# A decoder trunk on one core: groups of a projection unit no longer chained to the unit ahead, and three measured durations in the planner

## The chip, the cores and the metric

The kernel runs on one core of a Trainium2 chip. The metric is device time in microseconds (us), the median of several executions. Beside it there is one profiled execution with its trace; times "at 103.77" are us from the start of that trace's span. TensorE is called PE, its weight loads PEld, VectorE DVE, ScalarE ACT, GpSimd POOL, and the engine that issues the DMAs SP.

## The reference

Two layers over 256 tokens of width 1024. A layer normalises its input, multiplies it by one wide matrix (9808 columns), runs three causal attention mixers of 8 heads of 64 over the result, gates and projects each, merges them and adds the output projection to the residual.

```
for layer in range(2):
    h = rms_norm(x, gain)
    proj = h @ w_in                                # 1024 x 9808
    qa,ka,va,ga, qb,kb,vb,gb, qc,kc,vc,gc, q_idx,k_idx,w_idx, f_logit, merge = split(proj)
    oa = softmax(rope(qa) rope(ka)^T / 8 + causal) va * silu(ga)
    ob = the same for b, over the 64 keys that the indexer (q_idx, k_idx, w_idx) selects
    oc = the same for c without rope, with a bias of summed log_sigmoid(f_logit)
    merged = sum over n of sigmoid(merge[n]) * (o[n] @ w_branch[n])
    x = x + merged @ w_out
out = rms_norm(x, final_gain)
```

## The kernel before

Every fp32 product is made of three matmuls of rounded parts: an operand is split into a high part (`hi`, a copy on ACT) and the rest (`lo`, a subtraction on DVE), and hi x hi, hi x lo and lo x hi are summed in one PSUM bank. Weights come by DMA into one of three `raw` buffers; a piece of 128 columns (or of 2 rows of 128 by 512) is split into `wh` and `wl`, each a ring of six buffers.

The work is written as **units**. A unit of `unit_b` multiplies 128 columns of `w_in` by the transposed input `hTh`/`hTl` (256 tokens): 24 matmuls of 256 columns into one of three `proj` banks, 16 that need only `wh` and 8 that need `wl`. `unit_a` (values `v..`, output projection `o..`) and `unit_y` (branch projections `y..`) have 24 and 12 matmuls. Names: `ka2` is the key unit of mixer a for the pair of heads 2, `ga2` its gate unit, `qc2`, `gc2` likewise for mixer c; `m06` is a merge gate; `o00` and `o01` are the first two output units. A unit is issued in **groups** (`mm_ops`): before, 8, 5, 8 and 3 matmuls in `unit_b`, with `wl` needed from the second group on.

Between the units PE does the attention steps of a pair: the scores (`qk`, `scores`, six matmuls into both `s` banks), two sets of three transposes of the softmaxed scores (`pT`), and the product with the values (`av`). What they need is made on ACT and DVE: head-wise copies of queries and keys (`write_q`, `write_bd`, 64 partitions high), the maximum scan (L651), the exponential (L655), the normalisation (L663 on ACT or L666 on DVE), the copies of the transposes (L681, L683).

The order on every engine is made by a **planner** (`Plan.run`) while the program is built. Each operation has its tokens read and written, a key (its unit's number) and a duration from a formula. The planner takes the engine that can begin something first, and on it the operation that can begin first; among those that can begin at that moment, the lowest key. What it takes is fixed: the engines run their lists in order and wait by semaphores. Buffers of a ring are given in the order in which they are first named.

In the kernel before, every `mm_ops` call that belongs to a unit also writes one token, `k_main`, so that each group follows the group ahead of it, over unit borders too:

```
pe(emit, cost * n, reads, writes + ([k_main] if main else []), key, name)
```

Of the kernel before, what the change touches and what calls it, by code (L numbers as in the profile page):

```python
# [11 lines left out]
AF = mybir.ActivationFunctionType  # L12
# [3 lines left out]
S = 256  # L16
# [20 lines left out]
       ("ACT", "PE"): 170.0, ("DVE", "PE"): 200.0, ("POOL", "PE"): 170.0,  # L37
       ("DVE", "DVE"): 127.0, ("ACT", "ACT"): 127.0, ("POOL", "POOL"): 100.0, ("ACT", "SP"): 1500.0, ("DVE", "SP"): 1500.0}
SEM = 70.0
HALF = 95.0  # L40
SPLIT_LEAD = 2.0
MARGIN = 200.0
QK_MARGIN = 1000.0
# [3 lines left out]
DMA_KEY = (-95, -94, -85, -84)  # L47
HI_KEY = (-60, -48, -47, -46)
NB1 = 2
EARLY = 1.5  # L50
HT_KEY = (-50, -49.5, -46.8, -46.2)
BANKS = ("proj", "s", "t", "o")
# [176 lines left out]
def t_mm(n):  # L229
    return 1.3 + 0.4434 * n  # L230
# [3 lines left out]
def hybrid_trunk(ctx, tc, x, norm_gain, w_in, forget_bias, w_branch, w_out, final_gain, consts, out):  # L234
    nc = tc.nc
    PE, ACT, DVE, POOL = nc.tensor, nc.scalar, nc.vector, nc.gpsimd
# [17 lines left out]
    def pe(fn, cost, reads, writes, key, name="", margin=0.0, touch=()):  # L254
        o = plan.op([("PE", cost, fn)], reads, writes, key, 0.0, name, touch)
        o.margin = margin
        return o
# [52 lines left out]
    ncs = pool.tile([128, 2, 8], F32, name="ncs")  # L310
    widx = pool.tile([128, 2, 8], F32, name="widx")

    k_id, k_rope, k_gT, k_bdz, k_cst, k_fb, k_wf, k_widx, k_lf, k_cs, k_main = (Tok() for _ in range(11))
    k_cT, k_row = Tok(), [Tok() for _ in range(6)]
    k_isc = [Tok() for _ in range(2)]
    k_selb = [Tok() for _ in range(2)]
# [83 lines left out]
            dve(lambda: DVE.scalar_tensor_tensor(lo(), src(), scale, hi().bitcast(F32), op0=ALU.mult,  # L400
                                                 op1=ALU.subtract), n, reads + [wh], [wl], key, name, port=not ps)

    def mm_ops(o, terms, cost, writes, key, name, first, last, main=False):

        n = len(terms)

        def emit():
            for i, (a, b, _) in enumerate(terms):
                PE.matmul(o(), a(), b(), start=first and i == 0, stop=last and i == n - 1)  # L409
        reads = list({id(r): r for t in terms for r in t[2]}.values())  # L410
        pe(emit, cost * n, reads, writes + ([k_main] if main else []), key, name)

    units = [0]

# [6 lines left out]
    def unit_b(name, get, npart=128):  # L421
        u = unit(name)
        p = get(u)
        ps = Buf("proj")
        o = lambda: T(ps)[:npart, :S]
        his = [(lambda k=k: p[0].v[:, k], lambda k=k, h=h: h[:, k], [p[0]] + hT_all[i])
               for k in range(KC) for i, h in enumerate((hTh, hTl))]
        los = [(lambda k=k: p[1].v[:, k], lambda k=k: hTh[:, k], [p[1]] + hT_all[0]) for k in range(KC)]
        g = his[:8] + los[:2] + his[8:11] + los[2:5] + his[11:] + los[5:]
        for a, b in ((0, 8), (8, 13), (13, 21), (21, 24)):  # L430
            mm_ops(o, g[a:b], t_mm(256), [ps], u, name, a == 0, b == 24, True)
        return u, ps

    def unit_a(name, gets, t, ah, al, ra, c=0, n=512):
        u = unit(name)
        ps = Buf("proj")
        o = lambda: T(ps)[:, :n]
        for i in range(4):
            p = gets[i](u)
            g = []  # L440
            for k in (2 * i, 2 * i + 1):
                wh = lambda p=p, k=k: p[0].v[:, k % 2, c:c + n]
                g += [(lambda k=k: ah(k, t), wh, [p[0]] + ra[0](k)), (lambda k=k: al(k, t), wh, [p[0]] + ra[1](k))]
            for k in (2 * i, 2 * i + 1):
                wl = lambda p=p, k=k: p[1].v[:, k % 2, c:c + n]
                g += [(lambda k=k: ah(k, t), wl, [p[1]] + ra[0](k))]
            mm_ops(o, g, t_mm(n), [ps], u, name, i == 0, i == 3, True)
        return u, ps

    def rope(ps, key, np_=128):  # L450
# [119 lines left out]
    def write_q(src, n_ps, key, scale=None, name="q"):  # L570

        q = Buf("qh"), Buf("qx"), Buf("qy")
        up, dn = slice(0, 64), slice(64, 128)
        split_to(lambda: T(q[0]), lambda: T(q[2]), src[0], S, n_ps, [src[1]], q[0], q[2], key, scale, name)
        kx = [Tok(), Tok()]
        for t, o, a, b, i in ((q[1], up, q[0], up, 0), (q[1], dn, q[2], up, 1), (q[2], up, q[0], dn, None)):
            act(lambda t=t, o=o, a=a, b=b: ACT.activation(T(t)[o], T(a)[b].bitcast(F32), AF.Copy), S, False, [a],
                [q[2]] if i is None else [kx[i]], key, name, HALF, touch=[t])
        return q, kx

    def scores(q, k, ktoks, key, margin=MARGIN, shared=False):
        s0, s1 = Buf("s"), Buf("s")
        kt = [t for h in ktoks for t in h]
        q, kx = q

        def go():
            qh, x = T(q[0]), [T(q[1]), T(q[2])]
            kh, kl = T(k)
            for o, sl, n in ((T(s0)[:, :256], slice(0, 128), 128), (T(s1), slice(128, 256), 256)):
                PE.matmul(o.rearrange("p (h c) -> p h c", h=2), qh[:, sl], kl[:, :, :n], start=True, stop=False)  # L590
                for h in range(2):
                    PE.matmul(o[:, h * n:(h + 1) * n], x[h][:, sl], kh[:, 0 if shared else h, :n], start=False, stop=h == 1)  # L592
        pe(go, 3 * t_mm(256) + t_mm(512) + 216.0, [q[0], q[1], q[2], k] + kx + kt, [s0, s1], key, "qk", margin)
        return s0, s1

    class Pair:
# [44 lines left out]
        def attend(self, key):  # L641
# [31 lines left out]
            for h in range(2):  # L673
                ps = Buf("t")

                def tr(h=h, ps=ps):
                    for i in range(3):
                        PE.transpose(T(ps)[:, i * 128:(i + 1) * 128], T(es[h])[:, i * 128:(i + 1) * 128], ident)  # L678
                pe(tr, 330.0, ke[h] + [k_id], [ps], key, "pT", MARGIN, touch=[es[h]])
                src = lambda ps=ps: T(ps)[:, :384]  # L680
                act(lambda h=h, src=src: ACT.activation(T(ph)[:, h], src(), AF.Copy), 384, True, [ps],  # L681
                    [kp[h][0]], key, "pT", touch=[ph])
                dve(lambda h=h, src=src: DVE.tensor_tensor(T(pl)[:, h], src(), T(ph)[:, h].bitcast(F32), op=ALU.subtract),  # L683
                    384, [ps, kp[h][0]], [kp[h][1]], key, "pT", touch=[ph, pl])
# [41 lines left out]
    def write_bd(src, b, toks, key, ps, shared=False):  # L726

        up, dn = slice(0, 64), slice(64, 128)
        for h, o in enumerate((up, dn)):
            g, x = (0, up) if shared else (h, o)  # L730
            s = lambda x=x: T(src)[x, :S]
            hi = lambda x=x, g=g: T(b)[0][x, g]
            lo = lambda o=o, h=h: T(b)[1][o, h]
            if not (shared and h):
                act(lambda hi=hi, s=s: ACT.activation(hi(), s(), AF.Copy), S, ps, [src], [toks[g][0]], key, "bd", HALF, touch=[b])
                y = dn if x is up else up
                act(lambda hi=hi, y=y, g=g: ACT.activation(T(b)[0][y, g], hi().bitcast(F32), AF.Copy), S, False, [toks[g][0]],
                    [toks[g][1]], key, "bd", HALF, touch=[b])
            dve(lambda hi=hi, lo=lo, s=s: DVE.tensor_tensor(lo(), s(), hi().bitcast(F32), op=ALU.subtract), S,
                [src, k_bdz, toks[g][0]], [toks[h][2]], key, "bd", t_dve(S) + HALF, touch=[b], port=not ps)  # L740

# [125 lines left out]
    def unit_y(l, n, j, oi, gates, rank):  # L867
        u = unit(f"y{n}{j}")
        p = wbr(l, n, j, u)
        ps = Buf("proj")  # L870
        gh, gl = og[oi]
        cs = slice((j % 2) * 128, (j % 2) * 128 + 128)
        o = lambda: T(ps)[:, :S]
        g = []
        for k in range(4):
            wh, wl = lambda k=k: p[0].v[:, k, cs], lambda k=k: p[1].v[:, k, cs]
            g += [(wh, lambda k=k: gh[:, k], [p[0], k_og[oi][0][k]]), (wh, lambda k=k: gl[:, k], [p[0], k_og[oi][1][k]]),
                  (wl, lambda k=k: gh[:, k], [p[1], k_og[oi][0][k]])]
        g = [g[i] for i in (0, 1, 3, 2, 4, 5, 6, 7, 9, 10, 8, 11)]
        for a in (0, 6):  # L880
            mm_ops(o, g[a:a + 6], t_mm(256), [ps], u, f"y{n}{j}", a == 0, a == 6, True)
        ac = acc[:, j]
        if rank == 0:
            dve(lambda: DVE.scalar_tensor_tensor(ac, ac, 1.0, T(ps)[:, :S], op0=ALU.add, op1=ALU.mult), S,
                [ps], [k_acc[j]], u - EARLY, "y")
            return
        th = gates[n, j]
        t = th
        dve(lambda: DVE.scalar_tensor_tensor(T(t), T(t), 1.0, T(ps)[:, :S], op0=ALU.add, op1=ALU.mult), S,
            [ps], [t], u - EARLY, "y")  # L890
        plan.op([("DVE", t_dve(S), lambda: DVE.tensor_tensor(ac, ac, T(t), op=ALU.add)),
                 ("POOL", t_pool(S), lambda: POOL.tensor_tensor(ac, ac, T(t), op=ALU.add))], [t], [k_acc[j]], u, 0.0, "y").port = True
        if rank == 2:
            h, lo = merged(j)
            kh, kl = k_mg[j]
            split_to(lambda: h, lambda: lo, lambda: ac, S, False, [k_acc[j]], kh, kl, u, 0.5, "mg")
# [212 lines left out]
```

## Time and profile before

| | |
|---|---|
| median of 3 executions | 626.08 us (625.66 to 626.67) |
| the profiled execution | 625.54 us |
| its span in the trace | 623.6 us |
| PE busy | 612.1 us, 98% of the span, 4808 matmul records |
| PE weight loads | 584.8 us (94%) |
| DVE, ACT, POOL busy | 541.2 us (87%), 450.6 us (72%), 89.1 us (14%) |
| DMA | 107.32 MB, 172 GB/s in the mean |

PE's busy time counts a matmul from its start to a modelled end, and neighbours overlap: a matmul of 256 columns has a duration of 0.28 us but the next one starts some 0.11 us later. So a short wait of PE is to be read from the starts of neighbouring matmuls, not from the busy time.

### The profile page before, as it was taken

How to read it: one execution, taken by the hardware profiler on the slowest of the kernel's cores; microseconds unless marked ns; L12 is line 12 of the kernel's file. 1: busy time of each engine (PE TensorE's matmuls, PEld its weight loads, DVE VectorE, ACT ScalarE, POOL GpSimd, SP SyncE). 2: the span in 40 equal slices, each digit the busy share in tenths (PEclk: the TensorE clock that was granted, in tenths of full speed). 3: DMA queues.
4: the chain of work that ended last, by engine and by line, in shares of the span. 5: the costliest groups of instructions: out<-in, count | busy, mean ns of one | idle time of the engine just before them, and what ended most of it. 6: DMA issues, size and time to landing. Idle time of an engine off the chain costs nothing.

```text
span 623.6 us, 12663 instructions
## 1 busy us (share of the span) xinstructions
PE 612.1 (98%) x4808; PEld 584.8 (94%) x4808; DVE 541.2 (87%) x1328; ACT 450.6 (72%) x943; POOL 89.1 (14%) x100
## 2 busy tenths in 40 slices
PE   8999999999999999999999999999999999999996
PEld 6999999999998999999889999998999989999975
DVE  8899999975998899979589999998589978999673
ACT  5788498776886679855587867995679756987541
POOL 1242131000000223200005303200000013122001
PEclk9999999999999999999999999999999999999999
DMA  9954534586463653375455545457635465343811
GB/s 300 292 182 157 167 120 150 165 280 201 138 204 102 209 166 121 115 240 200 157 181 164 197 152 171 146 168 243 209 101 189 146 206 173 128 136 115 292 34 68
DMA packets 96156, 107.32 MB, mean 172 GB/s; under 512 B 4576, under 2 KB 84832, under 8 KB 96096
## 3 DMA queue, kind: packets, MB, share of 16 engines
q1 hardware_dynamic: 95808, 106.13, 52.3%
q8 instruction: 37, 0.61, 0.4%
q10 hardware_dynamic: 288, 0.39, 0.2%
q14 instruction: 23, 0.19, 0.1%
HBM read 103.37 MB, written 1.05 MB: 167 GB/s over the span
## 4 chain that ended last, share of the span: by engine, by line
PE 63%; DVE 23%; ACT 8%; issue 3%; DMA 2%; POOL 0%; POOLq 0%; DVEq 0%
PE proj L409 56%; DVE wl L368 7%; ACT wh L364 3%; DVE isc L842 2%; PE s L590 2%; PE s L592 1%; PE t L678 1%; PE proj L988 1%; DVE t L841 1%; DMA raw<-in_w_out_dram 1%; DVE rsh L454 1%; ACT pth L681 1%; ACT e L655 1%; DVE ptl L683 1%; DVE e L651 1%
## 5 line engine op out<-in xcount | busy, mean ns | idle before, releaser
L368 DVE TENSOR_TENSOR wl<-raw,wh 128x1024 fp32r<-128x1024 f32 (+1 forms) x190 | 239.5, 1269 | 40.9 <-ACT wh L364 40.2
L409 PE MATMUL proj<-hTh,wh 128*128 128x256 f32 (+1 forms) x1040 | 258.7, 278 | 0.5 <-DVE qy L400 0.2
L409 PE MATMUL proj<-hTl,wh 128*128 128x256 f32 (+1 forms) x1040 | 257.2, 277 | 0.0
L364 ACT ACTIVATE wh<-raw 128x1024 fp32r<-128x1024 f32 (+1 forms) x190 | 199.1, 1056 | 69.3 <-PE proj L409 59.1
L409 PEld LDWEIGHTS proj<-hTh,wh 128*128 128x128 f32 (+1 forms) x1040 | 194.7, 187 | 2.1 <-DVE rr L456 0.5
L409 PEld LDWEIGHTS proj<-hTl,wh 128*128 128x128 f32 (+1 forms) x1040 | 194.7, 187 | 0.3
L409 PE MATMUL proj<-hTh,wl 128*128 128x256 f32 (+1 forms) x1040 | 186.1, 281 | 1.1 <-DVE wl L368 0.9
L409 PEld LDWEIGHTS proj<-hTh,wl 128*128 128x128 f32 (+1 forms) x1040 | 147.7, 187 | 1.8 <-DVE wl L368 1.7
L455 POOL TENSOR_TENSOR rsh<-rsh,cst 128x256 f32<-128x256 f32 (+1 forms) x42 | 32.2, 768 | 392.8 <-DVE rsh L454 391.9
L655 ACT ACTIVATE e<-e,st 128x128 f32<-128x128 f32 x96 | 42.6, 448 | 6.0 <-DVE st L651 5.7
L457 POOL TENSOR_TENSOR rr<-rr,rsh 128x256 f32<-128x256 f32 (+1 forms) x42 | 45.4, 1082 | 7.4 <-DVE rr L456 2.7
L409 PE MATMUL proj<-wh,v 128*128 128x512 f32 (+1 forms) x144 | 35.8, 369 | 0.5 <-DVE v L400 0.5
L409 PE MATMUL proj<-og0l,wh 128*128 128x256 f32 x128 | 33.8, 276 | 0.0
L409 PE MATMUL proj<-og0h,wh 128*128 128x256 f32 x128 | 32.5, 278 | 0.0
L409 PE MATMUL proj<-wh,hTh 128*128 128x512 f32 x80 | 31.8, 398 | 0.0
L409 PE MATMUL proj<-wh,hTl 128*128 128x512 f32 x80 | 31.3, 391 | 0.0
L409 PEld LDWEIGHTS proj<-wh,v 128*128 128x128 f32 x144 | 25.2, 188 | 5.6 <-DVE v L400 0.9
L409 PE MATMUL proj<-og0h,wl 128*128 128x256 f32 x128 | 28.6, 276 | 0.0
L683 DVE TENSOR_TENSOR ptl<-t,pth 128x384 fp32r<-128x384 f32 x48 | 25.8, 554 | 0.8 <-ACT pth L681 0.4
L715 ACT ACTIVATE ot<-o 64x256 f32<-64x256 f32 x48 | 18.3, 382 | 11.0 <-PE o L695 10.4
L409 PE MATMUL proj<-wl,hTh 128*128 128x512 f32 x80 | 24.9, 392 | 0.0
L409 PEld LDWEIGHTS proj<-og0h,wh 128*128 128x128 f32 x128 | 24.0, 188 | 0.0
(195 smaller groups left out, 1057.1 us busy)
## 6 DMA issues: line engine op xcount, KB each, us to landing
raw<-in_w_in_dram SPq DMA_DIRECT2D x74, 1024.0 KB, 5.1
raw<-in_w_branch_dram SPq DMA_DIRECT2D x24, 512.0 KB, 3.4
raw<-in_w_out_dram SPq DMA_DIRECT2D x8, 1024.0 KB, 6.5
tmp<-wf SPq DMA_DIRECT2D x16, 128.0 KB, 5.5
raw<-in_w_in_dram SPq DMA_DIRECT2D x3, 512.0 KB, 6.1
x<-in_x_dram SPq DMA_DIRECT2D x4, 256.0 KB, 4.1
raw<-in_w_in_dram SPq DMA_DIRECT2D x2, 320.0 KB, 5.3
out_dram<-tmp SPq DMA_DIRECT2D x2, 320.0 KB, 2.6
```

The lines of the kernel that those rows point to most:

```text
L364: ACT.activation(p[0].v, sel(c.v), AF.Copy)
L368: DVE.tensor_tensor(p[1].v, sel(c.v), p[0].v.bitcast(F32), op=ALU.subtract)
L409: PE.matmul(o(), a(), b(), start=first and i == 0, stop=last and i == n - 1)
L454: dve(lambda: DVE.stream_shuffle(T(sh)[:np_], a(), SWAP), S, [ps], [sh], key, "rope")
L455: gps(lambda: POOL.tensor_tensor(T(sh)[:np_], T(sh)[:np_], s[:np_], op=ALU.mult), S, [k_rope], [sh], key, "rope")
L457: gps(lambda: POOL.tensor_tensor(T(r)[:np_], T(r)[:np_], T(sh)[:np_], op=ALU.add), S, [sh], [r], key, "rope")
L590: PE.matmul(o.rearrange("p (h c) -> p h c", h=2), qh[:, sl], kl[:, :, :n], start=True, stop=False)
L592: PE.matmul(o[:, h * n:(h + 1) * n], x[h][:, sl], kh[:, 0 if shared else h, :n], start=False, stop=h == 1)
L655: act(lambda t=t, a=a, n=n, e=e, st=st: ACT.activation(T(e)[:, a:a + n], T(e)[:, a:a + n], AF.Exp, bias=T(st)[:, t:t + 1], scale=-1.0, acc ...
L683: dve(lambda h=h, src=src: DVE.tensor_tensor(T(pl)[:, h], src(), T(ph)[:, h].bitcast(F32), op=ALU.subtract), 384, [ps, kp[h][0]], [kp[h][1 ...
L715: act(lambda r=r, h=h: ACT.activation(T(t)[r], T(o)[64:, h * S:(h + 1) * S], AF.Copy), S, True, [o], [kt[h]], key, "og", HALF, touch=[t])
L842: dve(lambda o=o, t8=t8: DVE.match_replace(o, T(t8), o, TAKEN), n, [t8], [k_isc[i]], key + r * step, "top8")
```

## The change

`k_main` is gone: the groups of one unit still follow each other (they write one PSUM bank), but a group may now be taken ahead of a group of an earlier unit. Three durations of the planner are changed: half-height copies on ACT (from 95 ns over a formula to 18), three transposes (330 to 275 ns), and the scores (216 to 240 ns over a formula). The sequence of the 24 matmuls within a unit of `unit_b` stays, its groups are cut at 8, 12 and 18 in place of 8, 13 and 21. No instruction is added or taken away in number: 4788 matmuls stand in either program. Six normalisations are now given to ACT instead of DVE, and two additions to DVE instead of POOL. Line numbers behind line 50 rise by 1, behind `unit_b` by 5.

```diff
-HALF = 95.0
+HALF, HALF_ACT = 95.0, 18.0
...
+UNIT_ORDER = ((8, 2), (3, 3), (5, 3))
...
-    def mm_ops(o, terms, cost, writes, key, name, first, last, main=False):
+    def mm_ops(o, terms, cost, writes, key, name, first, last):
...
-        pe(emit, cost * n, reads, writes + ([k_main] if main else []), key, name)
+        pe(emit, cost * n, reads, writes, key, name)
...
-        g = his[:8] + los[:2] + his[8:11] + los[2:5] + his[11:] + los[5:]
-        for a, b in ((0, 8), (8, 13), (13, 21), (21, 24)):
-            mm_ops(o, g[a:b], t_mm(256), [ps], u, name, a == 0, b == 24, True)
+        g, i, j = [], 0, 0
+        for nh, nl in UNIT_ORDER:
+            g += his[i:i + nh] + los[j:j + nl]
+            i, j = i + nh, j + nl
+        n = UNIT_ORDER[0][0]
+        for a, b in ((0, n), (n, 12), (12, 18), (18, 24)):
+            mm_ops(o, g[a:b], t_mm(256), [ps], u, name, a == 0, b == 24)
...
-                [q[2]] if i is None else [kx[i]], key, name, HALF, touch=[t])
+                [q[2]] if i is None else [kx[i]], key, name, HALF_ACT, touch=[t])
...
-        pe(go, 3 * t_mm(256) + t_mm(512) + 216.0, [q[0], q[1], q[2], k] + kx + kt, [s0, s1], key, "qk", margin)
+        pe(go, 3 * t_mm(256) + t_mm(512) + 240.0, [q[0], q[1], q[2], k] + kx + kt, [s0, s1], key, "qk", margin)
...
-                pe(tr, 330.0, ke[h] + [k_id], [ps], key, "pT", MARGIN, touch=[es[h]])
+                pe(tr, 275.0, ke[h] + [k_id], [ps], key, "pT", MARGIN, touch=[es[h]])
```

In the order that the planner makes of it, a group stands ahead of a group of an earlier unit at five places (`ka2`, `ga3` and `m22` of the first layer, `o01` of either layer). At many more places an attention step has moved by one to four groups; runs of attention steps between projection groups number 88, before 74. Three places are shown.

First place, PE, first layer, at the gate unit `ga2` of mixer a (it writes `proj_159`; `wl_75` is the low part of its weights). Before, the scores of pair 2 (bank `s_163`) are followed at once by the group that needs `wl_75`:

```order
L592 MATMUL s_163<-bd0h,qx_83 128x256
L592 MATMUL s_163<-bd0h,qy_86 128x256
L409 MATMUL proj_159<-hTh,wl_75 128x256 x2
L409 MATMUL proj_159<-hTh,wh_68 128x256
L409 MATMUL proj_159<-hTl,wh_68 128x256
```

In the changed kernel that group stands behind the scores of pair 3, the first group of `ga3` (`proj_160`, `wh_63`) and the first transposes of pair 2:

```order
L410 MATMUL proj_160<-hTh,wh_63 128x256
L410 MATMUL proj_160<-hTl,wh_63 128x256
L683 MATMUL t_165<-cst,e_131 128x128 x3
L410 MATMUL proj_159<-hTh,wl_75 128x256 x2
L410 MATMUL proj_159<-hTh,wh_68 128x256
L410 MATMUL proj_159<-hTl,wh_68 128x256
L683 MATMUL t_164<-cst,e_132 128x128 x3
```

The scores of pair 2 have moved ahead of the whole unit `m21`, and on DVE the making of `wl_75` has moved behind the four maximum scans of pair 2, the second of two pairs of key copies, four reciprocals and two normalisations.

Second place, DVE, first layer, mixer c: the low parts of the keys of pair 2 (`bd1l`) and pair 3 (`bd2l`) and, between them, the low parts of weights. Before:

```order
L368 TENSOR_TENSOR wl_73<-raw_119,wh_66 128x1024
L739 TENSOR_TENSOR bd1l<-proj_160,bd1h 64x256 x2
L368 TENSOR_TENSOR wl_74<-raw_119,wh_67 128x1024
L739 TENSOR_TENSOR bd2l<-proj_161,bd2h 64x256 x2
L884 SCALAR_TENSOR_TENSOR acc<-acc,proj_159 128x256
L651 ISA e_131,st_139<-s_162,fb_143 128x128
```

In the changed kernel:

```order
L744 TENSOR_TENSOR bd1l<-proj_161,bd1h 64x256 x2
L369 TENSOR_TENSOR wl_73<-raw_119,wh_66 128x1024
L656 ISA e_131,st_139<-s_162,fb_143 128x128
L656 ISA st_139 128x1
L656 ISA e_131,st_139<-s_163,fb_143 128x256
L656 ISA st_139 128x1
L744 TENSOR_TENSOR bd2l<-proj_160,bd2h 64x256 x2
L889 SCALAR_TENSOR_TENSOR acc<-acc,proj_159 128x256
```

The first pair of key copies now stands ahead of a weight subtraction, the second behind one weight subtraction and two scans in place of two weight subtractions. On PE the scores of pair 2 have moved ahead of the two groups of `y04` by it. The second layer has the same piece.

Third place, PE, second layer, the output projection: `o00` and `o01`, whose last group (`wh_66`, `wl_73`) needs the merged columns that are made last. Before, the groups of `o00` (`proj_161`) stand in a row:

```order
L409 MATMUL proj_161<-wl_72,v_79 128x512 x2
L409 MATMUL proj_161<-wh_66,v_79 128x512 x4
L409 MATMUL proj_161<-wl_73,v_79 128x512 x2
L409 MATMUL proj_159<-wh_63,v_78 128x512 x4
L409 MATMUL proj_159<-wl_70,v_78 128x512 x2
```

In the changed kernel (`o00` in `proj_160`, `o01` in `proj_159`):

```order
L410 MATMUL proj_160<-wl_72,v_79 128x512 x2
L410 MATMUL proj_159<-wh_63,v_78 128x512 x4
L410 MATMUL proj_159<-wl_70,v_78 128x512 x2
L410 MATMUL proj_160<-wh_66,v_79 128x512 x4
L410 MATMUL proj_160<-wl_73,v_79 128x512 x2
```

The first group of `o01` has moved ahead of the last group of `o00`.

## Rows read from the trace of the kernel before

**Rows 1.** The page, busy time, share and instructions of each engine.

```profile
PE 612.1 (98%) x4808; PEld 584.8 (94%) x4808; DVE 541.2 (87%) x1328; ACT 450.6 (72%) x943; POOL 89.1 (14%) x100
```

**Rows 2.** One stretch: us; busy by engine (instructions); granted clock, DMA share, GB/s.

```profile
70.00:117.00 47.00, 45.92 (x392) 44.84 (x391) 46.27 (x141) 40.10 (x100) 10.67 (x12) 1.00 0.53 169
```

**Rows 3.** PE in order of time, full pace: start, us, instruction [idle before].

```profile
98.34 0.50 PE L409 MATMUL proj<-hTh,wl 128*128 128x256 f32 x3
98.68 0.28 PE L409 MATMUL proj<-hTh,wh 128*128 128x256 f32 x1
```

**Rows 4.** PE in order of time, unit ka2 of the first layer.

```profile
87.52 0.28 PE L409 MATMUL proj<-hTh,wh 128*128 128x256 f32 x1
...
88.35 0.28 PE L409 MATMUL proj<-hTl,wh 128*128 128x256 f32 x1
89.06 0.51 PE L409 MATMUL proj<-hTh,wl 128*128 128x256 f32 x2 [0.43 <-DVE wl L368]
```

**Rows 5.** PE in order of time, scores of pair 2, then unit ga2.

```profile
103.00 0.28 PE L592 MATMUL s<-bd0h,qy 128*128 128x256 f32 x1
103.77 0.50 PE L409 MATMUL proj<-hTh,wl 128*128 128x256 f32 x2 [0.50 <-DVE wl L368]
```

**Rows 6.** PE in order of time, y05, gc2, scores of pair 3, first layer.

```profile
180.88 0.39 PE L409 MATMUL proj<-og0h,wl 128*128 128x256 f32 x2
181.39 0.39 PE L409 MATMUL proj<-hTh,wh 128*128 128x256 f32 x1
181.61 0.28 PE L409 MATMUL proj<-hTl,wh 128*128 128x256 f32 x1
...
182.32 0.28 PE L409 MATMUL proj<-hTl,wh 128*128 128x256 f32 x1
182.60 0.38 PE L590 MATMUL s<-bd2l,qh 128*128 128x256 f32 x1
```

**Rows 7.** PE, the same place in the second layer.

```profile
484.27 0.38 PE L409 MATMUL proj<-hTh,wh 128*128 128x256 f32 x1 [0.15 <-DVE bd0l L739]
```

**Rows 8.** PE, three sets of transposes, of the first and the second layer.

```profile
111.67 0.55 PE L678 MATMUL t<-cst,e 128*128 128x128 f32 x3
...
393.46 0.85 PE L678 MATMUL t<-cst,e 128*128 128x128 f32 x3
...
395.28 0.84 PE L678 MATMUL t<-cst,e 128*128 128x128 f32 x3
```

**Rows 9.** PE in order of time, unit o00 of the second layer.

```profile
596.47 0.62 PE L409 MATMUL proj<-wl,v 128*128 128x512 f32 x2
596.93 0.85 PE L409 MATMUL proj<-wh,v 128*128 128x512 f32 x3
598.28 0.50 PE L409 MATMUL proj<-wh,v 128*128 128x512 f32 x1 [0.50 <-DVE v L400]
```

**Rows 10.** PE, its last row.

```profile
617.00 0.40 PE L409 MATMUL proj<-wl,v 128*128 128x256 f32 x2
```

**Rows 11.** ACT, groups by line and form: instructions, busy us, mean ns, idle before.

```profile
L737 ACT ACTIVATE bd0h<-bd0h 64x256 fp32r<-64x256 f32 x17 | 7.1, 415 | 0.4
...
L399 ACT ACTIVATE og0h<-ot 128x256 fp32r<-128x256 f32 x16 | 6.7, 416 | 6.6 <-DVE ot L720 6.5
```

**Rows 12.** DVE in order of time, before and behind the scans of pair 2.

```profile
103.64 0.84 DVE L739 TENSOR_TENSOR bd1l<-rr,bd1h 64x256 fp32r<-64x256 f32 x2
104.49 1.23 DVE L368 TENSOR_TENSOR wl<-raw,wh 128x1024 fp32r<-128x1024 f32 x1
105.64 0.28 DVE L651 CUSTOM_DVE_ANT_0 e<-s,cst 128x128 f32<-128x128 f32 x1
...
106.75 1.22 DVE L368 TENSOR_TENSOR wl<-raw,wh 128x1024 fp32r<-128x1024 f32 x1
107.88 0.41 DVE L659 RECIPROCAL st<-st 128x1 f32<-128x1 f32 x3
108.21 0.53 DVE L666 TENSOR_SCALAR e<-e,st 128x128 f32<-128x128 f32 x2
```

**Rows 13.** SP's queue in order of time, the first two bias rows.

```profile
69.16 1.34 SPq L566 DMA_DIRECT2D tmp<-wf  x2
```

More of the change, by code (lines that the diff above doesn't have):

```diff
@@ L311, in hybrid_trunk @@
     widx = pool.tile([128, 2, 8], F32, name="widx")
-    k_id, k_rope, k_gT, k_bdz, k_cst, k_fb, k_wf, k_widx, k_lf, k_cs, k_main = (Tok() for _ in range(11))
+    k_id, k_rope, k_gT, k_bdz, k_cst, k_fb, k_wf, k_widx, k_lf, k_cs = (Tok() for _ in range(10))
     k_cT, k_row = Tok(), [Tok() for _ in range(6)]
@@ L446, in unit_a @@
                 g += [(lambda k=k: ah(k, t), wl, [p[1]] + ra[0](k))]
-            mm_ops(o, g, t_mm(n), [ps], u, name, i == 0, i == 3, True)
+            mm_ops(o, g, t_mm(n), [ps], u, name, i == 0, i == 3)
         return u, ps
@@ L734, in write_bd @@
             if not (shared and h):
-                act(lambda hi=hi, s=s: ACT.activation(hi(), s(), AF.Copy), S, ps, [src], [toks[g][0]], key, "bd", HALF, touch=[b])
+                act(lambda hi=hi, s=s: ACT.activation(hi(), s(), AF.Copy), S, ps, [src], [toks[g][0]], key, "bd", HALF_ACT, touch=[b])
                 y = dn if x is up else up
                 act(lambda hi=hi, y=y, g=g: ACT.activation(T(b)[0][y, g], hi().bitcast(F32), AF.Copy), S, False, [toks[g][0]],
-                    [toks[g][1]], key, "bd", HALF, touch=[b])
+                    [toks[g][1]], key, "bd", HALF_ACT, touch=[b])
             dve(lambda hi=hi, lo=lo, s=s: DVE.tensor_tensor(lo(), s(), hi().bitcast(F32), op=ALU.subtract), S,
@@ L880, in unit_y @@
         for a in (0, 6):
-            mm_ops(o, g[a:a + 6], t_mm(256), [ps], u, f"y{n}{j}", a == 0, a == 6, True)
+            mm_ops(o, g[a:a + 6], t_mm(256), [ps], u, f"y{n}{j}", a == 0, a == 6)
         ac = acc[:, j]
```

## The prediction, made before the changed kernel ran

> **What bounds the kernel now.** I read the busy times first. PE is busy for 98% of the span, DVE for 87%, ACT for 72% [rows 1]. So only what shortens PE's list, or the waits inside it, can shorten the kernel. The clock is no part of it: the granted clock is 1.00, the upper of the two levels (2.4 GHz), even in the stretch in which PE waits most [rows 2].
>
> PE's busy time hides short waits, because each row lasts to a modelled end that overlaps the next. So I went on to the starts in order of time. At full pace three matmuls of 256 columns take 98.68 - 98.34 = 0.34 us, 0.113 each [rows 3]. After an interruption the pace is a little slower: seven take 88.35 - 87.52 = 0.83, 0.119 each [rows 4]. Whatever exceeds 0.12 from start to start is a wait. Seen so, these stand at places where the order changes:
>
> - `ka2`: 89.06 - 88.35 = 0.71, a wait of 0.59 for the low part of its weights from DVE [rows 4].
> - `ga2`: 103.77 - 103.00 = 0.77, a wait of 0.65 for the same kind of thing [rows 5].
> - `gc2`: two matmuls from 180.88 to 181.39 leave 0.27, the next start 0.10 more, and the scores behind it come 0.28 after the last, 0.16 too late [rows 6]. Together 0.53. The second layer has the same piece, there with DVE's read of the key bank as the releaser [rows 7]; I take 1.06 for both.
> - Two sets of transposes at 393.46 and 395.28 last 0.85 and 0.84, one in the first layer 0.55 [rows 8]: 0.59 for both.
> - `o00`: 598.28 - 596.93 = 1.35 for three matmuls of 512 columns. Two take 0.46 [rows 9], so three 0.69; the wait for the last merged columns is 0.66.
>
> Sum 3.55 us. Everything else between is PE at its pace, and PE's last row starts at 617.00 of 623.6 [rows 10]: the tail behind it (last residual, norm, store) is untouched and moves with PE's end. So 3.55 is about the most that a new order can bring.
>
> The stretch from 70 to 117 is special: DVE is busy 46.27 of 47.00 us [rows 2]. There, a new order cannot create DVE time; it can only choose who waits.
>
> **The change, part by part.** The number of matmuls, copies and DMAs is the same; moved cuts within a unit cost nothing by themselves, since the 24 matmuls keep their sequence. Everything is in the order.
>
> *The last group of `o00`.* It now stands behind the first group of `o01`: six matmuls of 512 columns, 6 x 0.23 = 1.4 us [rows 9]. The wait was 0.66, and `o01`'s weights are those that `o00` has just used. Nothing is late next. Gain 0.66, on the path of the end.
>
> *`gc2` in both layers.* The second pair of key copies, which frees the bank, stood on DVE behind two weight subtractions since the step before; now behind one and two scans. A subtraction is 106.75 to 107.88, 1.13 us; four scans 106.75 - 105.64 = 1.11, so two 0.55 [rows 12]. The bank is free 0.58 earlier than before, against a wait of 0.37. The scores of pair 2 move ahead of `y04`, 12 x 0.113 = 1.36 earlier, and their keys come 1.13 earlier: if they were just in time, up to 0.23 is waited there. I take 0.1. The scores of pair 3 wait for the scans of pair 2, which start earlier too. Gain 1.06 - 0.2 = 0.86.
>
> *`ka2` and `ga2`.* DVE now makes `ga2`'s low weights behind four scans (1.11), a pair of key copies (104.49 - 103.64 = 0.85), four reciprocals (three take 0.33, so 0.44) and two normalisations (0.53) [rows 12]: 2.93 later. One normalisation ahead of it goes to ACT, -0.26: 2.7. PE has ahead of that group the scores of pair 3 (1536 columns, as much as six matmuls, 0.68), the first group of `ga3` (8 x 0.113 = 0.91) and a set of transposes (0.3): 1.9. Taken alone, the wait at `ga2` would grow by 0.8. But what was late behind `ga2`, the scans, normalisations and transposes of pair 2, is then done, and PE finds its next steps ready. The ends are a loss of 0.8 and a gain of 0.59 + 0.65 = 1.24. DVE's own list in this stretch is shorter by one or two normalisations, and the two units whose first groups run early give PE work where it stood. I take a gain of 0.7, nearer to the upper end, because DVE's queue ends this stretch no later than before.
>
> *The transposes of the second layer.* Scores and transposes move up by one group there, DVE is as full. Ends 0 and 0.59; I take 0.4.
>
> *The planner's new durations.* In the trace a copy of 64 partitions lasts 415 ns and one of 128 partitions 416 [rows 11], so the surcharge of 95 ns was too much, and the plan thought ACT later than it is. That the plan now has ACT right is why attention steps move up; it has no price of its own. The six normalisations that go to ACT lie in the 28% of the span in which ACT is not busy [rows 1]; without that cover they would cost some 0.3 us each.
>
> *More alternations.* 88 runs of attention steps in place of 74. After each, PE runs at 0.119 in place of 0.113 for a while. Were it 20 matmuls each time, 14 x 20 x 0.006 = 1.7 us; at zero the runs fall into stretches that are slow already. I take 0.3.
>
> *SP's queue.* In either layer one weight load now stands behind two or three bias rows that were behind it. Two take 1.34 us [rows 13]. Three raw buffers and a ring of six hide that; without this cover it would cost 1.3 to 2 us a layer.
>
> *Banks.* At five places a unit is opened while the one ahead is unfinished, so two of three `proj` banks are held. `gc2` in the trace waits for a bank: 0.37 in the first layer, and DVE's read is named in the second [rows 6, 7]. The Trainium skill, page "Perfetto Trace Analysis", section "Optimizing Tensor Performance", says that independent groups should rotate through PSUM banks so that evacuation overlaps the next group's matmuls. The two rows agree that a bank not yet read stops PE; by that rule all five openings would pay, and the sum below would shrink to 0.5. By the rows I take nothing for them: the opened bank was last written three units back, and at the five places at least 18 matmuls lie between, where ahead of `gc2` there are two units of 12 that DVE must also read.
>
> Sum: 0.66 + 0.86 + 0.7 + 0.4 - 0.3 = 2.3 us. The profiled execution, 625.54, would become 623.2. It is 0.54 under the median; against the median of 626.08 the forecast is **623.7 us**.
>
> **The rivals.**
>
> *Waits that only move* (same). Steps that are moved up wait for their own inputs, since DVE and ACT are no faster. Then `ka2`, `ga2`, the transposes and `gc2`'s scores give nothing, the bank waits of `gc2` (2 x 0.37) are half kept, and `o00` remains: 0.66 + 0.4 - 0.3 = 0.8, 625.3. For it: DVE's 46.27 of 47.00 [rows 2]. Against it: key copies are moved up on DVE by the same amount as the scores on PE.
>
> *Bank waits* (same). Five openings at 0.37 each, 1.85 against the 2.3: 625.6. For it: rows 6 and 7. Against it: the matmuls that lie between at the five places.
>
> *Weights late at `ga2`* (slower). The 2.7 us by which DVE makes the low weights later are waited in full, because the scores and transposes put ahead wait for the same scans; and `ga3` and `m22`, whose low weights stand behind it, have spent their first groups, so one more subtraction, 1.13, is waited. 3.8 lost, 0.66 + 0.86 gained, 0.3 more for alternations: 626.08 + 2.6 = 628.7. It decides once the wait at `ga2` exceeds 0.65 by about 2.5. Against it: PE needs 1.9 for what stands ahead, and that was ready soon after in the kernel before.
>
> **How the numbers follow.** A measurement of this kernel can tell about 0.2%, 1.25 us, from no change: faster is under 624.8, slower over 627.3. Chances: the forecast 0.62 (by itself 622.3 to 624.8; it reaches the upper end if the 0.7 of `ka2` and `ga2` and the 0.4 of the transposes both fail), waits that only move 0.18, bank waits 0.09, weights late at `ga2` 0.11. The low end is the 3.55 of all waits and a few tenths for small ones not listed, 622.3; the high end takes in the two cases of no change and leaves the slow one out, 626.5. Faster 0.63, same 0.26, slower 0.11.
>
> **What would show it.** Right: `o00`'s seven rows without a gap; `gc2` starting 0.12 after `y05` in both layers; transposes of 0.55 near 393; PE's last row near 614.7. `ga2`'s low group will still wait, but the sum of starts over 0.12 between 85 and 117 should be at least halved. Wrong: a gap of over 2 us at `ga2`; gaps ahead of first groups with DVE's key copies or `y` reads as releasers (banks); gaps ahead of scores (inputs). If PE's gaps vanish and the time does not, the pace after interruptions is the cause.

## The result: 0.6% slower, and the profile after

The changed kernel takes **629.73 us** (median of 5 executions, 629.50 to 630.27) against 626.08 for the kernel before in the same comparison: a ratio of 1.0063, 95% interval 1.0049 to 1.0078. That is more than the 0.2% that can be told from no change. The forecast was 623.7, the range 622.3 to 626.5; both are missed on the slow side.

The profiled execution lasts 629.50 us, its span 627.2. The line of busy times, as in [rows 1]:

```profile
PE 612.6 (98%) x4808; PEld 585.8 (93%) x4808; DVE 543.8 (87%) x1324; ACT 453.1 (72%) x949; POOL 88.1 (14%) x98
```

Nothing moves here but a few us of DVE and ACT; the work is the same but for six normalisations that went from DVE to ACT and two additions that went from POOL to DVE. PE's last row starts at 620.55 where it was 617.00 [rows 10], so the loss lies ahead of it, in PE's list. The pieces of PE's list that the prediction spoke of, in order of time (y05 and gc2, [rows 6]; o00, at the place of its wait in [rows 9]; the end):

```profile
180.81 0.39 PE L410 MATMUL proj<-og0h,wl 128*128 128x256 f32 x2
181.04 0.28 PE L410 MATMUL proj<-hTh,wh 128*128 128x256 f32 x1
...
181.94 0.28 PE L595 MATMUL s<-bd2l,qh 128*128 128x256 f32 x1
...
601.26 1.08 PE L410 MATMUL proj<-wh,v 128*128 128x512 f32 x4
602.18 0.62 PE L410 MATMUL proj<-wl,v 128*128 128x512 f32 x2
...
620.55 0.40 PE L410 MATMUL proj<-wl,v 128*128 128x256 f32 x2
```

`gc2` starts 0.23 after two matmuls, with no wait; the scores come 0.11 after the last of its eight. In `o00` the four matmuls of 512 columns at the place where PE waited before take 602.18 - 601.26 = 0.92, 0.23 each, so that wait is gone too. What came in is in the view of PE's waits (us in total, times, longest):

```profile
PE s L595 <- DVE st L656: 2.0, 4, 0.9
PE proj L410 <- DVE g L624: 1.6, 2, 0.8
PE s L595 <- ACT tmp L815: 1.4, 1, 1.4
```

None of the three was in the list of before. The places (DVE's scans that hold the `s` banks, the gate's product that holds a `proj` bank, the relu copies of the indexer that hold an `s` bank):

```profile
102.32 0.28 PE L410 MATMUL proj<-hTl,wh 128*128 128x256 f32 x1
103.01 0.39 PE L595 MATMUL s<-bd1l,qh 128*128 128x256 f32 x1 [0.42 <-DVE st L656]
...
217.54 0.39 PE L410 MATMUL proj<-og1h,wl 128*128 128x256 f32 x2
218.72 0.39 PE L410 MATMUL proj<-hTh,wh 128*128 128x256 f32 x1 [0.80 <-DVE g L624]
...
347.31 0.28 PE L410 MATMUL proj<-hTh,wh 128*128 128x256 f32 x1
349.03 0.39 PE L595 MATMUL s<-bd1l,qh 128*128 128x256 f32 x1 [1.44 <-ACT tmp L815]
```

A matmul of 256 columns starts 0.11 behind its neighbour at full pace, so these are waits of 0.6, 0.95 and 1.6 us; within the same scores another 0.4 and 0.2 follow. One like the second stands at `kb0` of the second layer too, one like the first at 388.17 (1.1 with what follows). I counted all of PE's starts so, from the first key unit on: what a matmul starts later behind its neighbour than the pace of its kind. The sum was 11.2 us before and is 15.9 now, 4.7 more. The matmuls between the waits take 1.2 less, not more. That leaves 3.5 us, the shift of the last row.

### The profile page after: what moved, and what is told of

It reads as the page before. It is cut to its first block, busy times and chain, and to the rows that moved or that the text cites. A ratio compares the mean times of both kernels' runs of the same rounds, so it can differ in the third digit from the quotient of the medians.

```text
span 627.2 us, 12650 instructions
## 1 busy us (share of the span) xinstructions
PE 612.6 (98%) x4808; PEld 585.8 (93%) x4808; DVE 543.8 (87%) x1324; ACT 453.1 (72%) x949; POOL 88.1 (14%) x98
## 4 chain that ended last, share of the span: by engine, by line
PE 66%; DVE 17%; ACT 13%; issue 3%; POOL 1%; DMA 0%; POOLq 0%; ACTq 0%; DVEq 0%
PE proj L410 58%; DVE wl L369 5%; ACT wh L365 3%; PE t L683 2%; DVE isc L847 2%; ACT e L660 2%; ACT qx L582 1%; PE proj L993 1%; DVE t L846 1%; PE s L595 1%; PE s L597 1%; DVE rsh L459 1%; ACT qy L582 1%; ACT pth L686 1%; ACT e L668 1%
## 5 line engine op out<-in xcount | busy, mean ns | idle before, releaser
L462 POOL TENSOR_TENSOR rr<-rr,rsh 128x256 f32<-128x256 f32 (+1 forms) x42 | 46.9, 1119 | 8.5 <-DVE rr L461 4.9
L686 ACT ACTIVATE pth<-t 128x384 fp32r<-128x384 f32 x48 | 22.5, 483 | 2.6 <-PE t L683 1.7
L410 PEld LDWEIGHTS proj<-og0l,wh 128*128 128x128 f32 x128 | 24.0, 188 | 0.0
```

What stands on the lines that cost most here:

```text
L462: gps(lambda: POOL.tensor_tensor(T(r)[:np_], T(r)[:np_], T(sh)[:np_], op=ALU.add), S, [sh], [r], key, "rope")
```

## The experiments

Medians are of 5 to 12 executions. Each ratio is to the kernel before in the same group of runs: 626.08 us for the changed kernel, 625.1 to 625.6 for the others. "Waits" is the sum of PE's late starts in the kernel's own trace, counted as above.

| kernel | median us | ratio to before (95%) | waits us |
|---|---|---|---|
| changed kernel | 629.73 | 1.0063 (1.0049 to 1.0078) | 15.9 |
| half95 | 624.60 | 0.9983 (0.9974 to 0.9991) | 11.4 |
| unchained_only | 624.75 | 0.9984 (0.9975 to 0.9992) | 11.5 |
| unchained_old_cuts | 624.72 | 0.9990 (0.9980 to 1.0001) | 10.3 |
| chained_half18 | 630.53 | 1.0080 (1.0066 to 1.0093) | 15.7 |
| pe_costs_only | 628.02 | 1.0036 (1.0023 to 1.0048) | 14.8 |
| transposes_only | 625.97 | 1.0016 (1.0006 to 1.0026) | 12.3 |
| scores_only | 630.29 | 1.0079 (1.0065 to 1.0092) | 14.9 |
| sbuf18_psum95 | 629.78 | 1.0067 (1.0054 to 1.0080) | 16.4 |
| sbuf60 | 622.66 | 0.9953 (0.9938 to 0.9967) | 9.4 |
| half_by_source | 622.25 | 0.9960 (0.9946 to 0.9974) | 8.4 |
| chained_by_source | 626.59 | 1.0023 (1.0013 to 1.0032) | 11.9 |
| tanh_first | 628.39 | 1.0053 (1.0039 to 1.0067) | 14.2 |
| after_pinned | 628.74 | 1.0047 (1.0034 to 1.0060) | 14.9 |
| scores_pinned | 629.55 | 1.0061 (1.0044 to 1.0077) | 13.7 |
| by_source_pinned | 620.73 | 0.9920 (0.9906 to 0.9934) | 7.1 |

### Which part of the change

Theory A: the 18 ns for half-height copies of ACT. Theory B: the groups that may leave their unit's place. Theory C: the new durations of PE.

`half95`, the changed kernel with the old surcharge:

```
-HALF, HALF_ACT = 95.0, 18.0
+HALF, HALF_ACT = 95.0, 95.0
```

> The changed kernel with the half-height copies back at the surcharge of 95 ns; unchained groups, the cut at 12 and 18, and the durations of scores and transposes stay. Theory A (the 18 ns are too few: in the trace a half-height copy from SBUF on ACT is followed by the next instruction 0.44 us later, not 0.33, so the plan puts attention steps too early and PE waits behind them): the loss is gone, 625 to 626.5 us, and no wait of over 1 us ahead of scores in the second layer. Theory B (the unchained groups or the new cuts cost the time): it stays at 629 to 630 us. Theory C (the durations of transposes and scores cost it): it stays at 629 to 630 us.

624.60, a little under the 625 expected: the whole loss is gone.

`chained_half18`, the kernel before with 18 ns alone (chain, cuts and PE's durations as before):

```
-HALF = 95.0
+HALF, HALF_ACT = 95.0, 18.0
```

> The kernel before with the surcharge of the half-height copies on ACT at 18 ns and nothing else: groups chained, old cuts, old durations of scores and transposes. Theory A: slow by itself, 628 to 630 us. Theories B and C: within 0.2% of 626.1 us.

630.53, a little over the 630 expected: the loss comes with the 18 ns, with the chain or without.

`unchained_only`, the kernel before without `k_main` and with the new cuts, and `unchained_old_cuts`, the same with the cuts of before:

```
-        pe(emit, cost * n, reads, writes + ([k_main] if main else []), key, name)
+        pe(emit, cost * n, reads, writes, key, name)
```

> The kernel before with unchained groups and the new cuts alone, all durations as before. Theory A: no loss, 624.5 to 626.5 us. Theory B: 628 to 630 us. Theory C: within 0.2% of 626.1 us.

> The kernel before without the chain of projection units, with the old durations and the old cuts after 8, 13 and 21 matmuls. With the new cuts this gave 624.75. If the gain of that run is the missing chain's: 624.3 to 625.2 here too. If it is the cuts': 625.3 to 626, as before.

624.75 and 624.72. B falls: without the chain the kernel is 0.1 to 0.2% faster, which is at the edge of what can be told, and the cuts do nothing to be seen.

`pe_costs_only`, then its two halves, the kernel before with

```
-                pe(tr, 330.0, ke[h] + [k_id], [ps], key, "pT", MARGIN, touch=[es[h]])
+                pe(tr, 275.0, ke[h] + [k_id], [ps], key, "pT", MARGIN, touch=[es[h]])
...
-        pe(go, 3 * t_mm(256) + t_mm(512) + 216.0, [q[0], q[1], q[2], k] + kx + kt, [s0, s1], key, "qk", margin)
+        pe(go, 3 * t_mm(256) + t_mm(512) + 240.0, [q[0], q[1], q[2], k] + kx + kt, [s0, s1], key, "qk", margin)
```

> The kernel before with the durations of transposes (275) and scores (240) alone. Theory A: within 0.2% of 626.1 us. Theory C: 628 to 630 us. Theory B: within 0.2%.

> The kernel before with transposes planned at 275 ns in place of 330, nothing else. The two new durations of TensorE alone gave 628.0. If the transposes' does it: 627.5 to 628.5, with the first transposes of a pair of heads waiting about 1 us, as in that run. If the scores' does it, or the two only together: 625 to 626.2.

> The kernel before with the scores planned 24 ns longer, nothing else. The transposes alone gave 625.97 us, both durations together 628.0. If the scores' duration carries the difference: 627 to 628.5. If only the two together lose time, which is then an accident of the order that they draw: 625 to 626.2.

The transposes alone change next to nothing (625.97). 628.02 and 630.29 were a surprise, the second above both ranges: 24 ns on a step of 0.8 us make the chained kernel 5 us slower, although the two durations together cost nothing without the chain (`half95` and `unchained_only` differ in them alone). So in these runs the size of a change to the planner's numbers says little; what it makes change places does. The trace of `scores_only` has one such place (ACT's rows, then PE's):

```profile
42.32 1.28 ACT L855 ACT_TABLE_LOAD   x1
43.62 0.38 ACT L855 ACTIVATE acc<-proj 128x256 f32<-128x256 f32 x1
43.90 0.59 ACT L811 ACTIVATE tmp<-s 128x512 f32<-128x512 f32 x1
```

```profile
42.65 0.28 PE L592 MATMUL s<-bd0h,qy 128*128 128x128 f32 x1
44.54 0.49 PE L590 MATMUL s<-bd0l,qh 128*128 128x512 f32 x1 [1.61 <-ACT tmp L811]
```

PE waits for a relu copy that stands behind a load of ACT's function table.

### What a half-height copy costs

In the trace of before I had read durations; now I read starts. ACT in order of time, near 214 us of the kernel before:

```profile
213.89 0.42 ACT L577 ACTIVATE qx<-qy 64x256 fp32r<-64x256 f32 x1
214.34 0.42 ACT L399 ACTIVATE qh<-rr 128x256 fp32r<-128x256 f32 x1
214.78 0.42 ACT L577 ACTIVATE qy<-qh 64x256 fp32r<-64x256 f32 x1
215.22 0.42 ACT L577 ACTIVATE qx<-qh 64x256 fp32r<-64x256 f32 x1
215.55 0.36 ACT L618 ACTIVATE th<-proj 128x256 f32<-128x256 f32 x1
```

All have the same duration, 0.42, but the starts are 0.45, 0.44, 0.44 and 0.33 apart: some are overlapped by the next instruction by 0.1 us, some not at all. Two kernels measured copies alone, in one execution each.

> Leaves out all of the reference's computation: ScalarE copies alone, twelve a block, 256 columns wide, nothing else running. Blocks: aa 128 partitions from SBUF, bb upper half to upper half, cc lower to lower, dd upper to lower, ee upper and lower in turn, ff crossing in turn, gg 128 partitions from PSUM, hh upper half from PSUM, ii halves from PSUM in turn, jj a half and a full one in turn. Theory A (a 64-partition copy from SBUF costs ScalarE more than a full one): start to start 0.44 us in bb to ff, 0.31 in aa, and 0.28 in gg, hh and ii; jj tells which copy of the two pays (0.44 behind the half one, 0.31 behind the full one, if the half one holds the engine). Rival A2 (in the kernel half-height copies wait for something else, the input or the shared port): 0.31 in bb and cc too. Rival A3 (only the copy that crosses from one half to the other is slow): 0.31 in bb, cc and ee, 0.44 in dd and ff.

Blocks of twelve, from first start to first start of the next (ACT in order of time):

```profile
4.35 3.78 ACT L40 ACTIVATE aa<-src 128x256 fp32r<-128x256 f32 x12 [2.34 <-DVE src L29]
8.04 3.76 ACT L40 ACTIVATE bb<-src 64x256 fp32r<-64x256 f32 x12
...
15.58 3.78 ACT L40 ACTIVATE dd<-src 64x256 fp32r<-64x256 f32 x12
19.37 5.10 ACT L40 ACTIVATE ee<-src 64x256 fp32r<-64x256 f32 x12
24.48 5.10 ACT L40 ACTIVATE ff<-src 64x256 fp32r<-64x256 f32 x12
29.59 3.42 ACT L40 ACTIVATE gg<-psrc 128x256 fp32r<-128x256 f32 x12
32.78 3.40 ACT L40 ACTIVATE hh<-psrc 64x256 fp32r<-64x256 f32 x12
35.95 4.79 ACT L40 ACTIVATE ii<-psrc 64x256 fp32r<-64x256 f32 x12
```

The full copies `aa` are (8.04 - 4.35) / 12 = 0.31 apart, the halves that stay in place, upper (`bb`) or lower (`cc`, left out above), (15.58 - 8.04) / 24 = 0.31 as well, and so are those that all cross (`dd`), but the halves that take turns (`ee`, `ff`) are (24.48 - 19.37) / 12 = 0.43 apart. From PSUM it is 0.27 in place (`gg`, `hh`) and 0.40 in turn (`ii`). My first form of theory A, that height itself costs, was wrong, and so was A3; of A2 only this held, that halves in place cost 0.31. The change of place costs.

> Leaves out all of the reference's computation: ScalarE copies (k blocks) and VectorE subtracts (v blocks) alone, twelve a block, 256 columns wide. The first run of copies alone showed 0.425 us start to start where copies of upper and lower halves take turns, and 0.315 for full ones, for halves that stay in place and for a half and a full one in turn from partition 0. Theory A4: a copy pays about 0.11 us more when the first partition that it reads or writes differs from that of the copy ahead of it. Blocks: ka full; kb source takes turns, output stays; kc output takes turns, source stays; kd full and lower half in turn; ke upper halves from SBUF and PSUM in turn; kf full ones from SBUF and PSUM in turn; kg the order up to up, up to down, down to up of the kernel; kh the order of the kernel's key copies, PSUM and SBUF in turn. A4: 0.425 in kd, and in kb or kc or both, near 0.315 in ka; ke and kf near the mean of 0.315 and 0.27. Rival A5 (only the alternation of both at once pays): 0.315 in kb and kc, 0.425 in kd. VectorE: if it has the same cost, vc is 0.1 us a piece above vb; if not, va, vb and vc agree.

```profile
8.05 5.09 ACT L40 ACTIVATE kb<-src 64x256 fp32r<-64x256 f32 x12
13.15 5.11 ACT L40 ACTIVATE kc<-src 64x256 fp32r<-64x256 f32 x12
18.27 5.10 ACT L40 ACTIVATE kd<-src 128x256 fp32r<-128x256 f32 x12
...
30.36 5.13 ACT L40 ACTIVATE kg<-src 64x256 fp32r<-64x256 f32 x12
```

```profile
9.28 4.10 DVE L45 TENSOR_TENSOR vb<-x,x 64x256 fp32r<-64x256 f32 x12
13.30 5.18 DVE L45 TENSOR_TENSOR vc<-x,x 64x256 fp32r<-64x256 f32 x12
```

It is enough that the source (`kb`) or the output (`kc`) changes its first partition, and a full copy pays as well when it follows a lower half (`kd`): 0.43. The kernel's own order of query copies, `kg`, pays every time. DVE has the same cost where source and output both take turns: 0.34 in place, 0.43 in turn (5.18 for twelve against 4.10). So 95 ns was about right for both engines, a little low for copies from SBUF (0.44 - 0.31 = 0.13 in the kernel). 18 ns holds only for copies from PSUM, and not for all: of the 16 in the trace of before that are followed at once by another instruction, 8 stand 0.285 ahead of it and 8 stand 0.38 to 0.41 ahead.

### Right durations

`half_by_source`, `chained_by_source` and `sbuf18_psum95` give the two kinds of copies surcharges of their own, the first and third in the changed kernel, the second in the kernel before; `sbuf60` has 60.0, 18.0:

```
-HALF, HALF_ACT = 95.0, 18.0
+HALF, HALF_SB, HALF_PS = 95.0, 135.0, 18.0
```

> The changed kernel with the surcharge that the trace shows for half-height ScalarE copies: 135 ns where the source is in SBUF (0.44 us start to start beside 0.31), 18 ns where it is PSUM. Theory A (the 18 ns for copies from SBUF lose the time): at or below the 624.6 us that 95 ns gave, 623.5 to 625, and no gap of 1 us ahead of the first groups of kb0. Rival (any other surcharge merely draws another order, and the sizes of the gaps are luck): anywhere from 624 to 630.

> The changed kernel with 18 ns for half-height copies from SBUF alone, and the old 95 ns for those from PSUM. Theory A (too short a price for the copies from SBUF loses the time): 628 to 631, like the changed kernel. Rival (too short a price of those from PSUM, or only both together): 623 to 625.5.

> The kernel before, chain, cuts and TensorE durations kept, with only the surcharges of half-height ScalarE copies changed, to 135 ns from SBUF and 18 ns from PSUM. Theory A (what the plan knows of these copies makes the difference, the chain little): 622.5 to 624. Rival (the 622.25 us came from the missing chain together with right surcharges): 624.8 to 626.

> The changed kernel with 60 ns from SBUF and 18 ns from PSUM. 18 ns from SBUF gave 629.8 (PSUM at 95) and 629.7 (PSUM at 18), 95 gave 624.6, 135 gave 622.25. Theory A as a steady effect of the surcharge: 625.5 to 628.5. If single orders are lucky or unlucky whatever the surcharge: outside of that.

622.25, 629.78, 626.59 and 622.66. In the changed kernel the price of copies from SBUF decides; 18 or 95 ns for those from PSUM makes no difference beside it. `half_by_source` came out below the range put down for it. Two expectations failed. With the chain, the same surcharges give no gain (626.59, above both ranges), so the 622.25 needs something else of the change too, the missing chain, the new cuts or PE's durations, which no run takes apart. And the effect is no slope: from 18 to 60 ns the time falls by 7.1 us, from 60 to 135 it stays. `sbuf60` lies outside the range of a steady effect, on the side that its expectation gave to orders that are lucky or unlucky whatever the surcharge. The planner is greedy, so a wrong duration costs nothing until it lets one step begin ahead of another.

### Two places followed to the end

*kb0.* ACT and then DVE of the changed kernel, ahead of the wait at 218.72:

```profile
216.02 1.06 ACT L365 ACTIVATE wh<-raw 128x1024 fp32r<-128x1024 f32 x1
216.99 0.36 ACT L623 ACTIVATE th<-proj 128x256 f32<-128x256 f32 x1
```

```profile
217.11 1.23 DVE L369 TENSOR_TENSOR wl<-raw,wh 128x1024 fp32r<-128x1024 f32 x1 [1.10 <-ACT wh L365]
218.25 0.42 DVE L624 SCALAR_TENSOR_TENSOR g<-th,proj 128x256 f32<-128x256 f32 x1
```

The gate's tanh `th` stands behind a weight copy of 1 us, its product `g` behind a subtraction of 1.1, and `g` holds the bank that `kb0` needs. With 18 ns the plan, by its own times, has ACT free 0.04 us before the tanh's input is ready, so the weight copy gets the place; with 60, 95 or 135 ns it can begin both at the same moment and takes the tanh, whose key is lower. `tanh_first` lets that one copy, in either layer, not begin for 0.15 us:

```
+                    if o.name in LATER:
+                        tt += 150.0
                     if bw is None or tt + w[1] < bw[0] + bw[1][1]:
```

> The changed kernel with one weight copy of ScalarE in each layer (the first piece of unit kb2's weights, at 216.02 us in the first layer) planned not earlier than 0.15 us after it could begin. The only differences in the order: in both layers the tanh of the gate unit gb1 stands ahead of that copy instead of behind it, and the gate's product on VectorE ahead of the piece's subtraction. Theory E (the 18 ns lose time by letting a copy of 1 us slip in ahead of a tanh whose bank PE needs): the waits of 1.05 us ahead of kb0 fall under 0.3 us in both layers, 627.5 to 628.3. Rival (the bank is late for another reason, as VectorE being full): the waits stay above 0.7 us, 629.3 to 630.

ACT and PE of `tanh_first`:

```profile
215.76 0.36 ACT L626 ACTIVATE th<-proj 128x256 f32<-128x256 f32 x1
216.15 1.06 ACT L368 ACTIVATE wh<-raw 128x1024 fp32r<-128x1024 f32 x1
```

```profile
217.40 0.39 PE L413 MATMUL proj<-og1h,wl 128*128 128x256 f32 x2
217.63 0.28 PE L413 MATMUL proj<-hTh,wh 128*128 128x256 f32 x1
```

Both waits are gone, and the time is 628.39, 1.34 below the changed kernel, just outside the 627.5 to 628.3 that was expected for 2 us of waits; a new one of 0.35 stands at 594 us.

*The table.* ACT of the changed kernel ahead of the wait at 349.03:

```profile
345.94 1.28 ACT L860 ACT_TABLE_LOAD   x1
347.24 0.38 ACT L860 ACTIVATE acc<-proj 128x256 f32<-128x256 f32 x1
347.65 1.06 ACT L365 ACTIVATE wh<-raw 128x1024 fp32r<-128x1024 f32 x1
348.61 0.36 ACT L815 ACTIVATE tmp<-s 128x256 f32<-128x256 f32 x1
```

The load comes with the first tanh after the logarithm. The plan counts it right behind the logarithm, some 10 us earlier (an empty step named "table"), and nothing at the tanh. The `pinned` kernels put a tanh of one column at the plan's place:

```
-        act(lambda: None, 0, False, [k_lf], [], key - 1, "table", 1190.0)
+        act(lambda: ACT.activation(tiny, half, AF.Tanh), 0, False, [k_lf], [], key - 1, "table", 1190.0)
```

> The changed kernel with one more ScalarE instruction, a tanh of one column into a tile that nothing reads, at the place where the plan counts the load of the tanh's table; the order of everything else is the same. Theory D (the load lands where the plan doesn't expect it, and PE's wait of 1.83 us for the scores at 349 us is its work): that wait is gone or under 0.6 us, and the time falls by 1.2 to 1.9 us, to 627.8 to 628.6. Theory A alone (the copies are the cause of that wait too): the wait stays above 1 us, 629.2 to 629.9.

> The kernel before with scores planned at 24 ns more (630.29 us) and the same extra tanh. Theory D: the wait of 1.82 us ahead of the scores at 44.5 us goes, 628.3 to 629.1. Without D: 630 to 630.6.

> The changed kernel with 135 ns from SBUF and 18 ns from PSUM (622.25 us), and the same extra tanh. In its trace no wait of PE above 0.2 us stands near either load, so theory D expects no gain that can be told: 621.7 to 622.5. If the load costs ScalarE time that reaches PE later, as at the scores at 384.7 us (1.22 us), 620.8 to 621.7.

The waits of 1.8 us went (in `scores_pinned` 0.4 is left), and in both a new one of 0.7 to 0.8 came at the scores near 345 us, so 1.0 and 0.7 us were gained where 1.2 to 2 were expected. The 0.7 is no more than the spread of the runs (628.47 to 630.70 against 629.42 to 631.66 of `scores_only`). In `by_source_pinned` it was 1.5 us, more than either range allowed: no wait had stood at the load, but one of 0.9 us at 365 us is gone, and one of 1.2 at the scores of 385 us is 0.9. With 620.73 this kernel is 0.8% faster than the one before. Its only wait of PE above 0.5 us between the start and the end of the program:

```profile
PE s L596 <- DVE st L657: 0.6, 1, 0.6
```

## Why the prediction was wrong

**The bound** was read rightly: PE at 98%, the granted clock 0.998 in the mean (0.999 before), and the time moved in the main with PE's waits (4.7 us more, 1.2 of them given back by the matmuls between).

**The step that failed** is *the planner's new durations*: "In the trace a copy of 64 partitions lasts 415 ns and one of 128 partitions 416, so the surcharge of 95 ns was too much", and "it has no price of its own". Equal durations are not equal costs. The starts in the same trace lie 0.44 and 0.31 apart where a copy changes its place and where it does not, so the plan was made wrong, not right: with 18 ns it is 0.11 us short at most copies from SBUF. This step alone cost 5.1 us (`half95`), and 7.5 against 135 ns (`half_by_source`), where the prediction put nothing.

That the 18 ns on copies from SBUF bring the loss is shown, with the chain and without. That they bring it because they are too short, and not because another number draws another order, is followed to the end at one place only, the tanh ahead of `kb0`. For the whole it is not shown: 60 ns are too short as well and lose nothing, and `scores_only` draws an order as slow with no copy's price touched.

The Trainium skill, page "VectorE: DVE Perf Modes", section "Two Vector instructions with no wait between them", says that an instruction whose input or output starts in another group of 32 partitions than the last one in that memory begins only when the earlier ones have finished. DVE's 0.43 against 0.34 agrees. The page says it of VectorE alone; ACT's blocks show the same. Had it been tried on ACT, that rule would have spoken against reading a price out of [rows 11].

**`gc2`** came as forecast, and by the mechanism: DVE's second pair of key copies there starts at 179.90 where it started at 180.48, 0.58 earlier, and the bank is free before PE asks for it. At `gc2` and its scores, 0.86 was put down. The late starts there (172 to 186 and 482 to 488 us) sum to 1.4 us before and 0.8 after: the scores that moved ahead of `y04` wait up to 0.2 each, and 0.6 is gained.

**`o00`** lost its wait of 0.66 as forecast, but by luck. In the trace of before, behind the matmul that waited [rows 9], come two of `wl` and then the next four of `wh`:

```profile
598.61 0.62 PE L409 MATMUL proj<-wl,v 128*128 128x512 f32 x2
599.08 1.09 PE L409 MATMUL proj<-wh,v 128*128 128x512 f32 x4
```

In the order printed for the third place of the change these two are `wl_72` and `wh_66`. So PE waited in the third of `o00`'s four groups, and the last group, which the change moves, did not wait. The third group stands ahead of `o01` in either kernel. In `chained_half18`, which has `o00` in a row as before, the same four matmuls do not wait either (603.49 - 602.57 = 0.92):

```profile
602.57 1.08 PE L409 MATMUL proj<-wh,v 128*128 128x512 f32 x4
603.49 0.62 PE L409 MATMUL proj<-wl,v 128*128 128x512 f32 x2
```

In the changed kernel DVE begins to write the column that PE had waited for at 599.10, more than 2 us ahead of its matmul; which part of the order brought that was not followed.

**`ka2` and `ga2`**, put at a gain of 0.7, lost: the late starts between 85 and 117 us go from 2.3 to 2.6. The low group of `ga2` waits 0.4 where it waited 0.65, but the scores of pair 2 wait 1.0 for banks (at 103.01). **The transposes** near 393 wait no longer, but the scores at 388 and 412 and the transposes at 414 wait 1.1, 0.8 and 0.6: from 380 to 420 us the late starts go from 1.4 to 3.3. That the 18 ns cause these is argued from `sbuf60` (none at 103 and 388; 0.7 at 409 remains), not followed step by step, and for the scores at 412 it is doubtful: `unchained_only`, with 95 ns, waits about 1 us at the same scores (409.56).

**The alternations** cost nothing that shows (the matmuls between the waits take less time, not more), and **SP's queue** does not show: no wait of PE above 0.3 us names a DMA. Of the rivals, *bank waits* was nearest in kind and wrong in place and price: 2 x 1.0 us at `kb0`, behind a late tanh, not 5 x 0.37 at the units opened early. *Weights late at `ga2`* named a time close to the measured one for a reason that does not hold: that group's wait is 0.17 in the view. Not one of the rivals questioned the numbers that the plan was given.

What the chain itself is worth is 0.9 us with the old durations (`unchained_only`), where my sum for the order was 2.3. Why the chained kernel loses 5 us by 24 ns on the scores and the unchained one nothing is open: one wait of 1.8 us stands at the table load, and forcing that load early gave back 0.7 us, within the spread of the runs (`scores_pinned`).

## What to carry to other kernels

Take an engine's price of an instruction from start to start, among its real neighbours, never from its recorded duration: a duration hides how much of it overlaps the next. In a kernel whose order a greedy planner draws, test every number of the planner by itself, the obvious ones too, because a wrong 0.1 us costs nothing until a step of 1 us slips in ahead of one on which the bound engine waits. Let a plan count an implicit cost where the machine pays it, or make the machine pay it where the plan counts it.

## What the hardware showed that I had not expected

- ACT and DVE lose their overlap, about 0.11 us on ACT and 0.1 on DVE for 256 columns, when neighbouring instructions take turns between partition 0 and partition 64. On ACT the source alone or the output alone is enough (0.43 against 0.31); on DVE only both together were measured (0.43 against 0.34). No other first partition was tried. On ACT 64 partitions cost no more than 128 (0.31 us each), a crossing from one half to the other nothing by itself, and nor do turns between SBUF and PSUM at the same partition (0.31 behind a copy from SBUF, 0.26 behind one from PSUM, `kf` of `act_starts`).
- A table load of 1.28 us was paid at the first tanh, not behind the logarithm where the plan counted it. The Trainium skill, page "ScalarE: Activation LUTs", section "What ACT_TABLE_LOAD costs", gives 1283 ns, which agrees, and a drain of 1380 ns beside it; here the next instruction starts 1.30 us after the load's start (347.24 - 345.94, and 43.62 - 42.32 in `scores_only`), so no such drain shows in the time of these two switches.
